# One level of Strassen's algorithm in the last output projection of a two-layer trunk, with weight sums made by GpSimd's DMAs

## Chip, cores and metric

The kernel runs on one core of a Trainium2 chip, in fp32. The metric is the device time of one execution in microseconds (us), the median of three runs. The engines are named as in the profile: PE is TensorE (PEld its weight loads), DVE VectorE, ACT ScalarE, POOL GpSimd, SP SyncE, whose queue issues DMAs.

## Reference

```python
x1 = x + gated_deltanet(rmsnorm(x, w0), ...)          # layer 0
# layer 1, Mamba-2 SSD mixer on h = rmsnorm(x1, w1):
#   z, xBC, dt = split(h @ w_in); xBC = silu(causal_conv(xBC))
#   chunked state-space scan (chunks of 128 tokens, 32 heads in 8 groups) -> y
#   y = grouped_rmsnorm(y * silu(z))                   # 1024 x 2048
x2 = x1 + y @ w_out                                    # w_out 2048 x 1024
out = rmsnorm(x2, final_w)                             # 1024 x 1024
```

1024 tokens, model width 1024, inner width 2048. The change concerns the last `y @ w_out` and what stands around it.

## The kernel before

Every large product is made from two fp32r pieces of each operand: `split` (L86, L87) writes a high piece with ACT (`scalar.copy`) and the remainder with DVE (`tensor_tensor` subtract), and three matmuls (high·high, high·low, low·high) go into one PSUM bank. A tile scheduler sorts the instructions of each engine by its own estimate; each engine then runs its list in order and waits on semaphores. Tiles come from pools with tags; a tag's buffers go round, so a new tile waits until the old one of its buffer has been read. All DMAs are issued by SP.

**Scan of layer 1.** The outer loop runs over groups g = -1 to 7. In each group 8 slots take one step of `scan(g)`, which treats one chunk n of 128 tokens, and one step of the projections and convolutions of group g+1 (`conv_halves`, whose halo COPY and MEMSET of 3 columns are POOL's L196 and L194). In a scan step `prep` uses POOL for `xw` (L861) and `t2` (L871), and `main` uses it for `S` (L887) and for the 1/rms of the group norm, `so` (L907, L909); DVE then makes `yn` (L910), PE turns `yn` in the next step's `store` (L66), ACT scales it to `yg` (L921) and SP stores it to `y1d` (L923). Where g = 7, there is no next group, and the matmuls of `out_proj` fill PE between the last steps.

**Output projection.** `out_proj` runs over halves nh of 512 output columns and 8 token tiles n; each of the 16 passes sums 16 tiles of 128 rows of w_out into one bank: 16 x 16 x 3 = 768 matmuls (L347 to L349) of 128x512. The weight pieces (`woh`, `wol`) of a half stay in SBUF; `y` is loaded and split in both halves (`yr`, `yh`, `yl`, 64 loads). In half 0 the sum with the residual `xin` (L353) is stored to DRAM (`xfd`); in half 1 it is loaded again, ACT sums the squares (L107, L113), POOL makes 1/rms (L115, L116), DVE scales the row (L119), and it is stored (L990). Layer 0 ends with the same function.

The next `with` opens a pool in the memory that the scan's pool has just left, and what is written there waits for its last readers:

```python
    with tc.tile_pool(name="nrm2", bufs=2) as nrm:
        nw = load_nw(nrm, final_norm_w)
        ...
        out_proj(yd1, sw_out, lambda n: x1d[n], (apool, bpool), nrm, nw, rows_last, xfd)
```

## Time and profile before

| what | value |
|---|---|
| median of 3 runs | 1995.43 us (1994.64 to 2000.03) |
| the profiled execution, its own time | 1990.66 us |
| its span, first to last instruction | 1989.0 us |
| mean granted clock of TensorE | 0.987 |
| PE busy | 1919.1 us, 96% |
| DVE busy | 1305.7 us, 66% |
| POOL busy | 411.6 us, 21% |

The span is 1.66 us shorter than the execution's own time, and that execution is 4.77 us faster than the median of the runs. PE's busy time counts a matmul from its start to its modelled end; matmuls overlap, so a group's mean (some 395 ns for 128x512) is longer than the distance from one to the next.

### The profile page before, as it was taken

The numbers are of one execution on the slowest core, as the hardware profiler recorded it, in microseconds if no ns is written. First come the engines' busy times: TensorE is split into PE (matmuls) and PEld (weight loads), VectorE is DVE, ScalarE is ACT, GpSimd is POOL, SyncE is SP. The second block draws the span as 40 slices with busy tenths as digits, with TensorE's granted clock in tenths as the row PEclk, the third lists the DMA queues.
The fourth block names the chain that finished last, engine by engine and source line by source line (L and its number), as shares of the span: only waits on it lengthen the run. The fifth ranks groups of instructions, "written<-read, shape, count | busy, mean of one in ns | idle before, by whom it ended". The sixth has DMA issues, their size and how long they took to land.

```text
span 1989.0 us, 36043 instructions
## 1 busy us (share of the span) xinstructions
PE 1919.1 (96%) x12974; PEld 1639.7 (82%) x12974; DVE 1305.7 (66%) x2915; ACT 1063.4 (53%) x2893; POOL 411.6 (21%) x818
## 2 busy tenths in 40 slices
PE   7997999999999999999999999999999999999998
PEld 5786888888888888897778788888888888888886
DVE  6797685778677776844354676657666676767333
ACT  5635656575656666564343554544555555555332
POOL 1101211212122212100000032423333243332000
PEclk9997999999999999999999999999999999999999
DMA  4421323232232323235574232222222223236654
GB/s 141 117 54 49 98 56 84 67 78 75 57 93 52 99 49 105 58 94 157 152 221 133 64 91 80 69 84 80 64 80 57 80 75 83 78 104 195 203 170 142
DMA packets 284789, 193.35 MB, mean 97 GB/s; under 512 B 65425, under 2 KB 246338, under 8 KB 284610
## 3 DMA queue, kind: packets, MB, share of 16 engines
q1 hardware_dynamic: 284610, 191.05, 34.2%
q8 instruction: 102, 1.67, 0.4%
q14 instruction: 77, 0.63, 0.1%
HBM read 159.34 MB, written 31.65 MB: 96 GB/s over the span
## 4 chain that ended last, share of the span: by engine, by line
PE 75%; DMA 9%; DVE 7%; ACT 4%; POOL 2%; issue 2%; SPq 1%; POOLq 0%; DVEq 0%; ACTq 0%
PE ps_proj L165 9%; PE ps_proj L166 9%; PE ps_proj L167 9%; PE ps_proj L347 6%; PE ps_proj L349 6%; PE ps_proj L348 5%; PE ps_proj L227 5%; PE ps_proj L228 4%; PE ps_proj L229 4%; DMA gcrow<-gcr_s 2%; PE ps_tr L66 2%; PE ps_pt L66 2%; DMA X<-xd 2%; DVE acc L204 2%; PE ps_sc L895 1%
## 5 line engine op out<-in xcount | busy, mean ns | idle before, releaser
L165 PE MATMUL ps_proj<-hid_h,wh 128*128 128x512 f32 x1024 | 412.9, 403 | 3.4 <-ACT acc L200 3.2
L167 PE MATMUL ps_proj<-hid_h,wl 128*128 128x512 f32 x1024 | 404.9, 395 | 0.0
L166 PE MATMUL ps_proj<-hid_l,wh 128*128 128x512 f32 x1024 | 403.6, 394 | 0.0
L227 PE MATMUL ps_proj<-zh,hid_h 128*128 128x256 f32 x1024 | 300.5, 293 | 1.0 <-DVE z L234 1.0
L229 PE MATMUL ps_proj<-zh,hid_l 128*128 128x256 f32 x1024 | 295.4, 288 | 0.0
L228 PE MATMUL ps_proj<-zl,hid_h 128*128 128x256 f32 x1024 | 295.4, 288 | 0.0
L165 PEld LDWEIGHTS ps_proj<-hid_h,wh 128*128 128x128 f32 x1024 | 192.7, 188 | 43.9 <-ACT acc L200 4.0
L167 PEld LDWEIGHTS ps_proj<-hid_h,wl 128*128 128x128 f32 x1024 | 192.5, 188 | 40.3
L166 PEld LDWEIGHTS ps_proj<-hid_l,wh 128*128 128x128 f32 x1024 | 192.9, 188 | 35.4
L347 PE MATMUL ps_proj<-woh,yh 128*128 128x512 f32 x512 | 205.2, 402 | 4.6 <-ACT yh L86 3.2
L348 PE MATMUL ps_proj<-wol,yh 128*128 128x512 f32 x512 | 204.4, 400 | 0.8 <-DVE wol L87 0.7
L349 PE MATMUL ps_proj<-woh,yl 128*128 128x512 f32 x512 | 203.1, 399 | 0.8 <-DVE yl L87 0.7
L227 PEld LDWEIGHTS ps_proj<-zh,hid_h 128*128 128x128 f32 x1024 | 196.3, 192 | 6.0 <-DVE z L234 2.3
L228 PEld LDWEIGHTS ps_proj<-zl,hid_h 128*128 128x128 f32 x1024 | 196.4, 192 | 3.0
L229 PEld LDWEIGHTS ps_proj<-zh,hid_l 128*128 128x128 f32 x1024 | 196.4, 192 | 0.3
L204 DVE SCALAR_TENSOR_TENSOR acc<-raw,cw_ssd,acc 128x512 f32<-128x512 f32 x192 | 156.5, 815 | 45.2 <-ACT acc L202 42.5
L86 ACT CAST yh<-yr 128x512 fp32r<-128x512 f32 x128 | 79.1, 619 | 142.2 <-PE ps_proj L348 90.8
L87 DVE TENSOR_TENSOR yl<-yr,yh 128x512 fp32r<-128x512 f32 x128 | 89.0, 696 | 98.7 <-ACT yh L86 98.3
L204 DVE SCALAR_TENSOR_TENSOR acc<-raw,cw_gdn,acc 128x512 f32<-128x512 f32 x192 | 145.9, 761 | 11.8 <-ACT acc L200 10.2
L87 DVE TENSOR_TENSOR wl<-wr,wh 128x512 fp32r<-128x512 f32 x128 | 89.3, 698 | 68.3 <-ACT wh L86 67.7
L317 POOL TENSOR_SCALAR_AFFINE_SELECT gcrow<-gcrow 128x512 f32<-128x512 f32 x128 | 92.1, 722 | 197.1 <-DMA gcrow<-gcr_g 141.8
L676 POOL TENSOR_SCALAR so<-so,cq 128x2 f32<-128x2 f32 x64 | 27.3, 426 | 462.7 <-ACT yn L675 462.7
(240 smaller groups left out, 3872.0 us busy)
## 6 DMA issues: line engine op xcount, KB each, us to landing
wr<-in_gdn_w_in_dram SPq DMA_DIRECT2D x96, 256.0 KB, 3.0
wr<-in_ssd_w_in_dram SPq DMA_DIRECT2D x96, 256.0 KB, 2.9
gcrow<-gcr_g SPq DMA_DIRECT2D x64, 256.0 KB, 3.6
yr<-y0d SPq DMA_DIRECT2D x64, 256.0 KB, 3.4
gcrow<-gcr_s SPq DMA_DIRECT2D x64, 256.0 KB, 3.9
yr<-y1d SPq DMA_DIRECT2D x64, 256.0 KB, 3.2
y0d<-yg SPq DMA_DIRECT2D x64, 128.0 KB, 1.9
wr<-in_gdn_w_out_dram SPq DMA_DIRECT2D x32, 256.0 KB, 3.5
```

Of the source, the lines that this page charges most:

```text
L87: nc.vector.tensor_tensor(out=lo, in0=src, in1=hi.bitcast(F32), op=ALU.subtract)
L165: nc.tensor.matmul(pt[0:nco], hi[:, j, 0:nco], xh[:, j, :], start=first, stop=False)
L166: nc.tensor.matmul(pt[0:nco], hi[:, j, 0:nco], xl[:, j, :], start=False, stop=False)
L167: nc.tensor.matmul(pt[0:nco], lo[:, j, 0:nco], xh[:, j, :], start=False, stop=last)
L204: nc.vector.scalar_tensor_tensor(out=acc, in0=raw[:, k:k + 512], scalar=cw[:, k * 32 + ti:k * 32 + ti + 1], in1=acc, op0=ALU.mult, op1=ALU ...
L227: nc.tensor.matmul(pt, xh, zh[:, k, :], start=k == 0, stop=False)
L228: nc.tensor.matmul(pt, xh, zl[:, k, :], start=False, stop=False)
L229: nc.tensor.matmul(pt, xl, zh[:, k, :], start=False, stop=k == KT - 1)
L317: nc.gpsimd.affine_select(out=t, in_=t, pattern=[[0, 4], [1, P]], compare_op=ALU.is_ge, fill=-1e30, base=0, channel_multiplier=-1)
L347: nc.tensor.matmul(pt, yh[:, j, :], hi[:, j, :], start=first, stop=False)
L348: nc.tensor.matmul(pt, yh[:, j, :], lo[:, j, :], start=False, stop=False)
L349: nc.tensor.matmul(pt, yl[:, j, :], hi[:, j, :], start=False, stop=last)
```

## The change

Layer 0 keeps the old function under the name `out_rows`. Layer 1's projection is cut into quarters: tokens into halves t, y's 2048 columns into halves k, the output columns into halves c. Instead of 8 products of quarters it makes 7 products of sums of quarters (Strassen's algorithm in Winograd's form), each of 8 steps j over 128 rows, with 4 token tiles p of 12 matmuls in a step: 7 x 8 x 12 = 672 matmuls (L427 to L429).

- **Weight sums.** `weight_sums` writes four sums of w_out's quarters to DRAM tiles `wo_ss1` to `wo_ss4`. It uses 44 DMAs issued by POOL, from DRAM to DRAM, 256x512 (512 KB) each: 16 copies (L358) and 28 that add to what is there (L360). One is issued per scan slot from group 0 on.
- **Products 0 and 1** (`early`) stand in slots 4 to 7 of group 7, with pieces in the pool of the old weight pieces. For product 1 POOL subtracts two loads of y (`N1`, L391, 8 times). ACT copies the 8 results from PSUM to `M` (L456).
- **Products 2 to 6** (`rest`) stand after the scan, in the pool `nrm2`, with rings of 4 for each piece. Products 2 and 6 make their y operand `Tt` with DVE (L394, 16 times), product 4 makes it with POOL (L387, 8 times). Results are added to the rows `xrow`, which are kept in SBUF: by POOL (`put_u`, L479, 20 times) and DVE (`put_u` 4, `grow` L482 8, `put` L473 and L475 12 times). The residual's 16 half rows are loaded over the steps of products 2 and 3 (L465).
- The store and reload of `xfd` are gone. `y1d` is laid out in four tiles, and y is loaded as 128x512.

```diff
+    def weight_sums(w_out, nm, which):
+        X = lambda c, k: w_out[k * 1024:(k + 1) * 1024, c * 512:(c + 1) * 512]
+        parts = {"s1": ((1, 0), (1, 1)), "s2": ((1, 0), (1, 1), (0, 0)), "s3": ((0, 0), (1, 0)),
+                 "s4": ((0, 1), (1, 0), (1, 1), (0, 0))}
+        forms = {f"x{c}{k}": X(c, k) for c in range(2) for k in range(2)}
+        parts = {f: parts[f] for f in which}
+        for f in parts:
+            forms[f] = tc.dram_tile([1024, 512], F32, name=f"wo_{nm}{f}")
+        def steps():
+            for q in range(4):
+                r = slice(q * 256, (q + 1) * 256)
+                for i in range(4):
+                    for f, p in parts.items():
+                        if i < len(p):
+                            src, dst = X(*p[i])[r, :], forms[f][r, :]
+                            if i == 0:
+                                d = nc.gpsimd.dma_start(dst, src)
+                            else:
+                                d = nc.gpsimd.dma_start(dst, src, accum_op=ALU.add)
+                            tc.keep_in_program_order(d)
+                            yield
+        return forms, steps()
...
+    def out_proj(yd, X, made, resid):
+        tok = lambda t, p: p + 4 * (1 - t)
+        wf = ("x00", "s1", "s2", "x01", "s3", "s4", "x11")
+        U = lambda: [ps_proj(), ps_proj(), ps_pt(), ps_pt()]
+        V = lambda: [ps_tr(), ps_tr(), ps_sc(), ps_sc()]
+        def load_y(k, t, j, tag="acc"):
+            yr = cv.tile([P, 515], F32, tag=tag, name="yr", bufs=3)[:, 0:512]
+            nc.sync.dma_start(yr, yd[k, 1 - t][j * P:(j + 1) * P, :])
+            return yr
+        def y_form(i, j, Tt):
+            if i in (0, 3, 5):
+                return load_y(*{0: (0, 0), 3: (1, 0), 5: (1, 1)}[i], j)
+            if i == 4:
+                a, b = load_y(1, 1, j), load_y(0, 1, j, "raw")
+                nc.gpsimd.tensor_tensor(out=a, in0=a, in1=b, op=ALU.subtract)
+                return a
+            if i == 1:
+                a, b, d = load_y(0, 0, j), load_y(0, 1, j, "raw"), N1[j // 4][:, j % 4, :]
+                (nc.gpsimd if made else nc.vector).tensor_tensor(out=d, in0=a, in1=b, op=ALU.subtract)
+            else:
+                a, d = load_y(*{2: (1, 1), 6: (1, 0)}[i], j), Tt[:, j, :]
+                nc.vector.scalar_tensor_tensor(out=d, in0=N1[j // 4][:, j % 4, :] if i == 2 else d, scalar=-1.0, in1=a,
+                                               op0=ALU.mult, op1=ALU.subtract)
+            return d
...
+        def pieces(i, j, ring, Tt):
+            raw = w_form(wf[i], j)
+            wh, wl, yh, yl = ring(j)
+            split(wh, wl, raw)
+            split(yh, yl, y_form(i, j, Tt))
+            return wh, wl, yh, yl
+        def mac(pt, pc, p, first, last):
+            wh, wl, yh, yl = pc
+            c = slice(p * P, (p + 1) * P)
+            nc.tensor.matmul(pt, yh[:, c], wh, start=first, stop=False)
+            nc.tensor.matmul(pt, yh[:, c], wl, start=False, stop=False)
+            nc.tensor.matmul(pt, yl[:, c], wh, start=False, stop=last)
+        def product(i, banks, ring, Tt=None):
+            for j in range(KT):
+                pc = pieces(i, j, ring, Tt)
+                for p in range(4):
+                    mac(banks[p], pc, p, j == 0, j == KT - 1)
+                yield
...
+        def early():
+            M.extend(apool.tile([P, 4, 512], F32, tag="a0", name="M", bufs=2) for _ in range(2))
+            N1.extend(apool.tile([P, 4, 512], F32, tag="a1", name="N1", bufs=2) for _ in range(2))
+            for i in range(2):
+                banks = U()
+                yield from product(i, banks, in_a(("a2", "a3") if made else ("a2",)))
+                for p in range(4):
+                    nc.scalar.copy(M[i][:, p, :], banks[p])
+        def rest(npool, nw, on_rows, before_last=lambda: None):
+            rows = {t: [npool.tile([P, D], F32, tag="xr", name="xrow", bufs=NT) for _ in range(4)] for t in range(2)}
+            Tt = npool.tile([P, 8, 512], F32, tag="T", name="Tt", bufs=1)
+            u, m = M
...
+            def ring(j):
+                return [npool.tile([P, 512], F32R, tag=t, name=t, bufs=4) for t in ("woh", "wol", "yh", "yl")]
+            def put(t, p, c, pt, op):
+                v = half(t, p, c)
+                if op == ALU.add:
+                    nc.vector.tensor_tensor(out=v, in0=pt, in1=v, op=ALU.add)
+                else:
+                    nc.vector.tensor_tensor(out=v, in0=v, in1=pt, op=ALU.subtract)
+            def put_u(t, p, c, op, of=u, eng=nc.gpsimd):
+                v = half(t, p, c)
+                eng.tensor_tensor(out=v, in0=v, in1=of[:, p, :], op=op)
+            def grow(p, pt):
+                nc.vector.tensor_tensor(out=u[:, p, :], in0=pt, in1=u[:, p, :], op=ALU.add)
...
+            def d01():
+                for p in range(4):
+                    put_u(0, p, 0, ALU.add)
+                for p in range(4):
+                    put_u(1, p, 1, ALU.subtract, m, nc.vector)
+                    put_u(1, p, 0, ALU.add, m)
+            def d2(p, pt):
+                grow(p, pt)
+                put_u(1, p, 0, ALU.add)
+            def d3(p, pt):
+                put(0, p, 0, pt, ALU.add)
+                first(0, p, 0)
+            def d4(p, pt):
+                grow(p, pt)
+                put_u(1, p, 1, ALU.subtract)
+                first(1, p, 1)
+                put_u(0, p, 1, ALU.subtract)
+            def d5(p, pt):
+                put(1, p, 0, pt, ALU.add)
+                finish(1, p, 0)
+            for i, done in ((2, d2), (3, d3), (4, d4), (5, d5)):
+                banks = V() if i % 2 else U()
+                for j, _ in enumerate(product(i, banks, ring, Tt)):
+                    if i == 2 and j < 6:
+                        for q in range(2 * j, 2 * j + 2):
+                            fetch(*((0, q, 0), (1, q - 4, 1), (1, q - 8, 0))[q // 4])
+                    if (i, j) == (2, 6):
+                        d01()
+                    if i == 3 and j < 4:
+                        fetch(0, j, 1)
+                if i == 5:
+                    before_last()
+                for p in range(4):
+                    done(p, banks[p])
+            banks = U()
+            for j in range(4):
+                pc = pieces(6, j, ring, Tt)
+                for p in range(4):
+                    mac(banks[p], pc, p, j == 0, False)
+            pcs = [pieces(6, j, ring, Tt) for j in range(4, KT)]
+            for p in range(4):
+                for j in range(4):
+                    mac(banks[p], pcs[j], p, False, j == 3)
+                put(0, p, 1, banks[p], ALU.subtract)
+                finish(0, p, 1)
...
+    def y_cut(yd, g, n):
+        return yd[g // 4, n // 4][(g % 4) * 256:(g % 4 + 1) * 256, (n % 4) * P:(n % 4 + 1) * P]
...
             for slot in range(8):
+                if g >= 0:
+                    next(steps1, None)
+                if g == 7 and slot > 3:
+                    next(early1)
+                    next(early1)
                 next(S, None)
+                if g == 7 and slot > 3:
+                    next(early1)
                 next(J, None)
             flush()
+            if g == 7:
+                next(early1)
+                next(early1)
             next(S, None)
+            for _ in early1 if g == 7 else ():
+                pass
+    bctx.close()
...
-        out_proj(yd1, sw_out, lambda n: x1d[n], (apool, bpool), nrm, nw, rows_last, xfd)
+        rest1(nrm, nw, rows_last)
```

The instructions move as follows. POOL, in one slot of group 0 of layer 1's scan, from the 1/rms of one chunk (`so`) to that of the next. Before:

```order
L909 TENSOR_TENSOR so_14272<-so_14272,expo_82 128x1
L196 COPY raw_14437<-raw_14316 128x3
L194 MEMSET raw_14565 128x3
L887 TENSOR_TENSOR S_14497<-S_14381,egl_s_13351 128x256
L871 TENSOR_TENSOR t2_14464<-xs_13459,dskip_327 128x256
L907 TENSOR_SCALAR so_14400<-so_14400 128x1
```

The same place after the change:

```order
L1140 TENSOR_TENSOR so_14269<-so_14269,expo_82 128x1
L215 COPY raw_14435<-raw_14313 128x3
L360 DMA wo_ss3_343<-in_ssd_w_out_dram 256x512
L213 MEMSET raw_14564 128x3
L360 DMA wo_ss4_344<-in_ssd_w_out_dram 256x512
L1118 TENSOR_TENSOR S_14496<-S_14379,egl_s_13343 128x256
L1102 TENSOR_TENSOR t2_14463<-xs_13451,dskip_327 128x256
L1138 TENSOR_SCALAR so_14398<-so_14398 128x1
```

Two adding DMAs stand around the halo's MEMSET, ahead of `S`, `t2` and the next `so`. The 44 DMAs stand in 22 such pairs, one DMA a slot on the average, in groups 0 to 5. In two of the pairs (rows of `wo_ss4` behind rows of `wo_ss4`) the second adds to what the first has just added to, and waits for its landing.

PE, around the last transposes of the scan (`yn`, the last chunk of group 7). Before:

```order
L349 MATMUL ps_proj_21811<-woh_21639,yl_21869 128x512
L66 MATMUL ps_tr_21572<-ident_73,yn_21567 128x128 x2
L347 MATMUL ps_proj_21888<-woh_21585,yh_21891 128x512
L348 MATMUL ps_proj_21888<-wol_21586,yh_21891 128x512
L349 MATMUL ps_proj_21888<-woh_21585,yl_21892 128x512
```

After the change (`wy` are the pieces of product 1, `woh`, `wol`, `yh` and `yl` those of product 2):

```order
L427 MATMUL ps_proj_21760<-wy_21945 128x512
L66 MATMUL ps_tr_21936<-ident_73,yn_21859 128x128 x2
L428 MATMUL ps_proj_21760<-wy_21945 128x512
...
L429 MATMUL ps_pt_21762<-wy_21969 128x512
L427 MATMUL ps_proj_22011<-woh_22017,yh_22019 128x512
L428 MATMUL ps_proj_22011<-wol_22018,yh_22019 128x512
L427 MATMUL ps_proj_22012<-woh_22017,yh_22019 128x512
L428 MATMUL ps_proj_22012<-wol_22018,yh_22019 128x512
L427 MATMUL ps_pt_22013<-woh_22017,yh_22019 128x512
L428 MATMUL ps_pt_22013<-wol_22018,yh_22019 128x512
L429 MATMUL ps_proj_22011<-woh_22017,yl_22020 128x512
```

Where the old order goes on with matmuls whose operands are of the old pools, the new one has 20 matmuls of product 1 left, and then the first of product 2, whose pieces lie in the new pool.

DVE at the same place. Before:

```order
L903 TENSOR_TENSOR y_21560<-y_21560,z7_20965 128x256
L87 TENSOR_TENSOR wol_22061<-wr_22062,woh_22060 128x512
L910 TENSOR_SCALAR yn_21567<-y_21560,so_21566 128x256
L87 TENSOR_TENSOR wol_22061<-wr_22066,woh_22060 128x512
L87 TENSOR_TENSOR wol_22061<-wr_22070,woh_22060 128x512
L87 TENSOR_TENSOR yl_21892<-yr_21889,yh_21891 128x512
```

After the change:

```order
L1141 TENSOR_SCALAR yn_21859<-y_21852,so_21858 128x256
L87 TENSOR_TENSOR wy_21969<-N1_21437,wy_21969 128x512
L394 SCALAR_TENSOR_TENSOR Tt_22010<-N1_21436,yr_22023 128x512
L394 SCALAR_TENSOR_TENSOR Tt_22010<-N1_21436,yr_22050 128x512
L394 SCALAR_TENSOR_TENSOR Tt_22010<-N1_21436,yr_22077 128x512
L87 TENSOR_TENSOR wol_22018<-wr_22015,woh_22017 128x512
L87 TENSOR_TENSOR wol_22045<-wr_22042,woh_22044 128x512
L87 TENSOR_TENSOR wol_22072<-wr_22069,woh_22071 128x512
L87 TENSOR_TENSOR wol_22099<-wr_22096,woh_22098 128x512
L87 TENSOR_TENSOR yl_22020<-Tt_22010,yh_22019 128x512
```

Three sums and four weight remainders stand ahead of the first `yl` of product 2. `Tt`, `woh` and the rows are in the new pool, so the first write there on DVE, on ACT (`woh_22017`), on POOL (`xrow`, L479) and the load of `nw` on SP wait for the landing of the last stores of `y1d`, which read `yg` from the old pool. After that landing ACT's order is four `woh`, one copy to `M`, then `yh_22019`.

## Rows read from the trace of the kernel before

**Rows 1.** The page, sections 1 and 4: busy time, chain that ended last.

```profile
PE 1919.1 (96%) x12974; PEld 1639.7 (82%) x12974; DVE 1305.7 (66%) x2915; ACT 1063.4 (53%) x2893; POOL 411.6 (21%) x818
...
PE 75%; DMA 9%; DVE 7%; ACT 4%; POOL 2%; issue 2%; SPq 1%; POOLq 0%; DVEq 0%; ACTq 0%
```

**Rows 2.** Windows: PE, PEld, DVE, ACT, POOL busy (count), clock, DMA share, GB/s.

```profile
1200.00:1740.00 540.00, 536.33 (x3708) 461.21 (x3707) 358.13 (x658) 281.44 (x742) 180.48 (x331) 1.00 0.27 76
...
1795.50:1840.00 44.50, 44.50 (x253) 35.86 (x252) 34.15 (x65) 26.10 (x63) 7.93 (x16) 1.00 0.69 210
1840.00:1981.60 141.60, 141.60 (x615) 115.09 (x613) 54.90 (x83) 43.78 (x85) 7.22 (x22) 1.00 0.59 177
```

**Rows 3.** Chain of waits at the end: start, us, what.

```profile
1981.98 0.70 DVE xrow L359
...
1984.46 0.75 DVE xn L119
1985.22 0.66 DVEq L990
```

**Rows 4.** Groups by line, 1750 to 1989 us: busy, mean ns | idle before.

```profile
L87 DVE TENSOR_TENSOR yl<-yr,yh 128x512 fp32r<-128x512 f32 x64 | 45.0, 703 | 55.6 <-ACT yh L86 55.5
L86 ACT CAST yh<-yr 128x512 fp32r<-128x512 f32 x64 | 39.6, 619 | 72.6 <-PE ps_proj L348 57.2 <-issue 10.6 <-DMA yr<-y1d 3.1
L87 DVE TENSOR_TENSOR wol<-wr,woh 128x512 fp32r<-128x512 f32 x32 | 22.6, 727 | 11.6 <-ACT woh L86 11.4
...
L119 DVE SCALAR_TENSOR_TENSOR xn<-xrow,rr,nw 128x512 f32<-128x512 f32 x16 | 11.3, 748 | 10.2 <-POOL rr L116 10.2
...
L359 DVE TENSOR_TENSOR xrow<-ps_proj,xin 128x512 f32<-128x512 f32 x8 | 5.5, 692 | 14.3 <-PE ps_proj L349 14.3
```

**Rows 5.** Timeline, the scan's last store: start, us, engine line.

```profile
1837.40 0.38 PE L66 MATMUL ps_tr<-ident,yn 128*128 128x128 f32 x2
...
1839.21 0.61 ACT L921 ACTIVATE yg<-ps_tr,vecs 128x128 f32<-128x128 f32 x2
...
1839.92 0.42 SPq L923 DMA_DIRECT2D y1d<-yg  x1
```

**Rows 6.** DMA issues, 1200 to 1740 us: count, KB, median us to landing.

```profile
gcrow<-gcr_s SPq DMA_DIRECT2D x52, 256.0 KB, 3.9
y1d<-yg SPq DMA_DIRECT2D x50, 128.0 KB, 1.8
```

**Rows 7.** DMA issues, 1790 to 1989 us.

```profile
y1d<-yg SPq DMA_DIRECT2D x6, 128.0 KB, 3.4
```

**Rows 8.** Windows (as Rows 2) at the start of layer 0's output projection.

```profile
1008.90:1010.40 1.50, 0.13 (x2) 0.07 (x1) 0.09 (x1) 0.74 (x2) 0.00 (x0) 1.00 0.96 192
1010.50:1013.80 3.30, 3.30 (x8) 2.39 (x9) 1.80 (x3) 0.92 (x2) 0.00 (x0) 0.50 0.95 313
```

**Rows 9.** Timeline of POOL over one scan step: [idle before, releaser].

```profile
1363.70 0.10 POOL L194 MEMSET raw<- 128x3 f32 x1
1366.80 0.95 POOL L861 TENSOR_TENSOR xw<-xs,dtd_s 128x256 f32<-128x256 f32 x1 [3.00 <-PE ps_sc L882]
...
1368.34 0.61 POOL L871 TENSOR_TENSOR t<-xs,dskip 128x256 f32<-128x256 f32 x1
1370.92 0.19 POOL L907 TENSOR_SCALAR so<-so 128x1 f32<-128x1 f32 x1 [1.97 <-ACT yn L906]
```

**Rows 10.** Timeline of DVE's convolution sums while POOL is idle.

```profile
1407.12 2.33 DVE L204 SCALAR_TENSOR_TENSOR acc<-raw,cw_ssd,acc 128x512 f32<-128x512 f32 x3 [2.39 <-ACT acc L202]
```

**Rows 11.** Timeline, the same sums beside POOL's work.

```profile
1430.10 2.81 DVE L204 SCALAR_TENSOR_TENSOR acc<-raw,cw_ssd,acc 128x512 f32<-128x512 f32 x3
...
1430.22 1.12 POOL L317 TENSOR_SCALAR_AFFINE_SELECT gcrow<-gcrow 128x512 f32<-128x512 f32 x1
...
1431.31 1.05 POOL L861 TENSOR_TENSOR xw<-xs,dtd_s 128x256 f32<-128x256 f32 x1
```

**Rows 12.** View of the tile `so`, 1200 to 1750 us: who waited.

```profile
PE ps_tr L66: 3.6, 5
```

More of the change, by code (lines that the diff above doesn't have):

```diff
@@ L102, in rms_rows, with rms_first, rms_second, rms_first0 @@
         return xn
-    def rms_first(pool, xrow):
+    def rms_first(sq, xrow, c):
+        ss = st.tile([P, 2], F32, tag="ss8", name="ss8", bufs=NT)
+        nc.scalar.activation(sq, xrow[:, c * 512:(c + 1) * 512], AF.Square, accum_out=ss[:, 0:1])
+        nc.gpsimd.tensor_scalar(out=ss[:, 0:1], in0=ss[:, 0:1], scalar1=1.0 / D, scalar2=EPS, op0=ALU.mult,
+                                op1=ALU.add)
+        return ss
+    def rms_second(xrow, xn, ss, nw, emit, c):
+        cs = slice(c * 512, c * 512 + 512)
+        nc.scalar.activation(xn[:, cs], xrow[:, cs], AF.Square, accum_out=ss[:, 1:2])
+        r = st.tile([P, 1], F32, tag="rr", name="rr")
+        nc.gpsimd.tensor_scalar(out=r, in0=ss[:, 1:2], scalar1=1.0 / D, scalar2=ss[:, 0:1], op0=ALU.mult, op1=ALU.add)
+        nc.gpsimd.tensor_tensor(out=r, in0=r, in1=neg_half[:, 0:1], op=ALU.pow)
+        for kh in range(2):
+            cs = slice(kh * 512, kh * 512 + 512)
+            nc.vector.scalar_tensor_tensor(out=xn[:, cs], in0=xrow[:, cs], scalar=r, in1=nw[:, cs], op0=ALU.mult,
+                                           op1=ALU.mult)
+            emit(kh, xn[:, cs])
+    def rms_first0(pool, xrow):
         xn = pool.tile([P, D], F32, tag="xn", name="xn")
@@ L399, in hybrid_trunk, with y_dram @@
     dskip = bcast(ssd_d[0], 32, "dskip")
+    def y_dram(nm):
+        return {(k, t): tc.dram_tile([1024, 512], F32, name=f"{nm}{k}{t}") for k in range(2) for t in range(2)}
+    def y_cut(yd, g, n):
+        return yd[g // 4, n // 4][(g % 4) * 256:(g % 4 + 1) * 256, (n % 4) * P:(n % 4 + 1) * P]
     yd0 = [tc.dram_tile([2048, P], F32, name=f"y0d{n}") for n in range(NT)]
+    yd1 = y_dram("y1d")
+    wo1, steps1 = weight_sums(sw_out, "s", ("s1", "s2", "s3", "s4"))
+    early1, rest1 = out_proj(yd1, wo1, True, lambda n: x1d[n])
     with tc.tile_pool(name="gw", bufs=2) as gw:
@@ L785, in hybrid_trunk @@
                 z_weights(g + 1)
-    bpool = ctx.enter_context(tc.tile_pool(name="bpool", bufs=2))
+    bctx = ExitStack()
+    bpool = bctx.enter_context(tc.tile_pool(name="bpool", bufs=2))
     hid2 = hid_tiles(apool)
@@ L796, in rows_mid @@
             norm(lambda kh, xn: to_hid(kh, xn, hid2, n))
-        out_proj(yd0, gw_out, lambda n: x[n * P:(n + 1) * P, :], (apool, bpool), nrm, nw, rows_mid, x1d)
-    yd1 = [tc.dram_tile([2048, P], F32, name=f"y1d{n}") for n in range(NT)]
-    xfd = [tc.dram_tile([P, D], F32, name=f"xfd{n}") for n in range(NT)]
+        out_rows(yd0, gw_out, lambda n: x[n * P:(n + 1) * P, :], (apool, bpool), nrm, nw, rows_mid, x1d)
     with tc.tile_pool(name="sw", bufs=2) as sw:
```

46 lines of the change are left out of this document (41 added, 5 removed).

## The prediction

> **What bounds the kernel now.** I read the page first: PE is busy for 96% of the span and holds 75% of the chain that ended last [rows 1]. The average hides stages, so I cut the end into windows [rows 2]. Up to 1740 us the scan of layer 1 keeps PE busy for 536.33 of 540 us; from 1795.5 us, where the projection's matmuls begin between the last scan steps, PE has no gap at all. From 1840 to 1981.6 us it issues 615 instructions in 141.6 us at the full clock of 1.00, which is 141.6 / 615 = 0.2302 us for each 128x512 matmul. In the same window DVE works for 54.9 us (39%), POOL for 7.2, DMA is at 0.59. So here only PE counts, and a matmul left out is worth 0.2302 us as long as all else keeps up. Last I read the chain's end [rows 3]: after the last matmul the row's last half passes DVE, ACT, POOL, DVE and SP from 1981.98 to the span's end at 1989.0, 7 us, which no matmul covers.
>
> **Matmuls.** 768 become 672: 96 x 0.2302 = **-22.1 us**. This is the whole gain; all other parts cost.
>
> **The handoff from product 1 to product 2.** Before, nothing is written to new memory at this point, and PE goes on without a gap. After, the first writes of product 2 wait for the landing of the scan's last store. Its time comes from two places. In the timeline the last transposes start at 1837.40, ACT's two `yg` end at 1839.82, and SP issues the store at 1839.92 [rows 5]: 2.5 us from transposes to issue, of which ACT is busy with splits for about 1.4, so 1.1 to 2.5. From issue to landing such a store takes 1.8 us in the scan [rows 6] and 3.4 us under the projection's loads [rows 7]. The landing S then lies 2.9 to 5.9 us after the transposes; I take 4.2, a little under the middle, since the loads of y for product 2 are mostly done by then. ACT needs six operations of 0.62 us [rows 4] from S to the end of the first `yh`: S + 3.7. PE has 20 matmuls left when the transposes are done, 20 x 0.23 = 4.6 us. The idle time is 4.2 + 3.7 - 4.6 = **+3.3 us** (2.0 to 5.0). DVE is not far behind: three `Tt` (the nearest row, L119, has 748 ns), four remainders of 727 ns and one of 703 give the first `yl` at S + 5.9; PE's order puts six matmuls without `yl` ahead, which covers 1.4 of those 2.2 us.
>
> What a pause like this does to the clock stands in layer 0, at the start of its projection: PE had only 0.13 us of work in 1.5 us, and the next 3.3 us ran at a granted clock of 0.50, that is at 1.2 GHz instead of 2.4 [rows 8]. 3.3 us at half speed lose about 1.7 us; a part of it falls together with the wait for `yl`, so the two give **+1.7 us** (0 to 3).
>
> **Feeding products 2 to 6.** They last 480 x 0.2302 = 110.5 us. DVE's work in them, by the rows of 4: 80 splits x 0.715 = 57.2; 16 `Tt` and 16 row scalings x 0.748 = 23.9; 24 sums of the size of L359 x 0.692 = 16.6; together 97.7 us, 88% where it was 39% in the window before. POOL makes 28 sums of 128x512. No such row is shown; the nearest is 0.61 us for a 128x256 sum [rows 9], so twice that, 1.2 us alone, 34 us in all. DVE and POOL slow each other: three convolution sums take 2.33 us while POOL is idle [rows 10], and 2.81 beside 2.17 us of POOL work [rows 11], 0.22 us for each us of POOL. That adds 34 x 0.22 = 7.5 us to DVE: 105 of 110.5 us. It still fits, but the load is uneven. In product 6 the eight `Tt`, 16 splits, eight scalings and four sums are 26 us against 22.1 of PE; rings of four steps and product 5's slack cover some of it. The DMAs are near their limit in product 2 as well: `nw` (0.5 MB) and six half rows (1.6 MB) are issued ahead of the fourth load of y, some 2.1 MB, or 6.7 us at the 313 GB/s that a full queue moved [rows 8], and after it every step wants 1 MB in 2.76 us. Between nothing, if the rings cover all of it, and 10 us, if product 6's excess of 4 and a DMA delay of some 6 both show, I take **+4 us**.
>
> The Trainium skill speaks against this part: by "SBUF — State Buffer", section "Who interferes with whom", DVE and GpSimd share one pair of ports as an exclusive lock, and a DVE instruction with two SBUF inputs contends with a GpSimd instruction that reads SBUF. The rows agree in kind (2.33 to 2.81 us), but show 0.22 of POOL's time and not all of it; what the whole lock would cost is rival 5.
>
> **Products 0 and 1 in the last slots.** Their 192 matmuls fill PE as the old ones did there. They need 32 splits, as many as the old stretch had for as many matmuls, but also 8 copies on ACT (5 us), 8 sums on POOL (9.6 us alone, beside a POOL that was busy for 7.93 of 44.5 us [rows 2]) and 24 loads of y. POOL's sums stand ahead of `so` of the last chunks. **+2 us** (0 to 6).
>
> **The 44 DMAs of POOL in the scan.** No DMA of POOL and no adding DMA is shown before. In a scan step POOL is idle for 3.00 us behind the halo's MEMSET, where a pair goes, and for 1.97 us before `so` [rows 9]. The nearest row for the issue itself is SP's, 0.42 us [rows 5]; by it a pair of 0.84 us is hidden, and so it is up to 1.5 us for each; the operations behind it (`xw`, `S`, `t2`) are needed late, but `so` leads to `yn`, to PE's transposes and to the next step. Two pairs have a second member that waits for the first one's landing: 3.9 us, if it is as long as the row of gcrow [rows 6]. Their 22.5 MB to read and as much to write join a DMA share of 0.27 [rows 2]. Lower bound 0; a gain is excluded, since nothing is taken away from the scan. Upper bound: every pair holds POOL as long as such a landing, 0.9 us longer than the idle stretch, 22 x 0.9 = 20 us. SP's issue is the row of the same kind, so I stay near the lower end: **+2 us**, the two waits (2 x 0.9).
>
> **The tail.** The last quarter's halves finish per token tile as before, with the sum, the square, 1/rms and the scaling in the same order [rows 3], but DVE has up to six scalings of earlier rows between. **+1 us** (0 to 2).
>
> **Sum.** -22.1 + 3.3 + 1.7 + 4 + 2 + 2 + 1 = -8.1. The sum is made against the profiled execution: 1990.66 - 8.1 = 1982.6 us. That execution lies 4.77 below the median of the runs, 1995.43, so the forecast for the median is **1987.4 us** (-0.4%).
>
> **Rivals.**
> 1. *Main case*, the sum above: 1982 to 1992 us, chance 0.46.
> 2. *DVE and the loads become the bound.* If product 6's excess shows whole (4), product 2 waits for DMA (6), and the early slots cost 6, the terms are -22.1 + 5 + 10 + 6 + 2 + 1 = +1.9; with a part of it covered, 1993 to 1998 us, no measurable change. For it: 105 of 110.5 us; against it: rings of four, and ACT and DMA have room on the mean. 0.21.
> 3. *Slower: POOL's DMA pairs delay `so`.* If a pair holds POOL for longer than the idle 3.00 us, the excess goes into `xw` and `so`, behind them into `yn` and PE's in-order transposes, 22 times. The gain is gone at 8.1 / 22 = 0.37 us per pair beyond the main case, and it is measurably slower from 0.64. At 1 us per pair: 1987.4 + 22 = 2009 us. For it: PE already waits for `yn` at five places, 3.6 us [rows 12]; against it: POOL was busy for just 180 of 540 us. 0.14. It could also come from DVE's side: if each DMA waited behind one DVE instruction of 0.75 us (L119's), a pair would be 1.5 us later, and the idle stretch would cover it only where an issue costs less than 0.75 us. The Trainium skill names this way ("SBUF — State Buffer", section "🔬 SBUF: two separate sides", its warning on DMAs issued from GpSimd): GpSimd writes their descriptors, and a DVE instruction in a two-port mode locks it out. No row of before has such a DMA.
> 4. *All is covered.* The handoff's 5 us remain, the rest is hidden: 1995.43 - 22.1 + 5 = 1978 us. 0.15.
> 5. *POOL blocks DVE wholly* in products 2 to 6 instead of for 0.22 of its time: 97.7 + 34 = 131.7 us of DVE, 21 us more than PE's 110.5, in place of the 4 us of the sum: 1987.4 - 4 + 21 = 2004 us. Against it: [rows 10, 11], where it is 0.48 us beside 2.17. 0.04.
>
> **Chances and range.** A measurement tells 0.3%, 6 us, from no change. Faster, below 1989.4: case 4 (0.15) and most of the main case (0.41): 0.56. Same: the rest of the main case (0.05) and case 2: 0.26. Slower: cases 3 and 5, 0.18. The range goes from case 4's 1977 to 2000, past case 2; what it leaves out is case 5, most of case 3 and a little below case 4, 0.2. The main case's own range is 1982 to 1992.
>
> **What would show it.** Right: 672 matmuls; a gap of 2 to 5 us of PE just before L427's first matmul of product 2, released by ACT's `yh`, then a clock of about 0.5 for a few us; products 2 to 6 in 110 to 121 us with DVE near 90%; the scan up to group 6 within 4 us of before. Wrong: PE idle before L66 with the release by `yn` in groups 0 to 5 (case 3), `xw` or `so` standing behind a POOL DMA; or gaps within products 2 to 6 ended by `yl`, `Tt` or a load of y (case 2).

## The result, and the profile after

The changed kernel takes 1981.46 us (median of 17 runs, 1979.31 to 1994.54), the kernel before, run beside it, 1996.43 (17 runs, 1987.66 to 2003.13). The ratio is 0.9933, 95% interval 0.9918 to 0.9948. The forecast was 1987.4 us, a gain of 8 us; the measured one is 13 us by the ratio, at the lower edge of the main case's 1982 to 1992 us.

The page of the profiled execution (1979.31 us, span 1977.5 us): busy time, the chain that ended last, the new queue, and POOL's DMAs with their median us to landing.

```profile
PE 1891.2 (96%) x12878; PEld 1616.0 (82%) x12878; DVE 1361.1 (69%) x2955; ACT 1072.4 (54%) x2917; POOL 508.3 (26%) x898
...
q0 software_dynamic: 9920, 23.07, 6.3%
...
PE 69%; DVE 10%; DMA 9%; POOL 4%; ACT 4%; issue 3%; SPq 0%; POOLq 0%; DVEq 0%; ACTq 0%
...
wo_ss<-in_ssd_w_out_dram POOLq DMA_DIRECT2D x44, 512.0 KB, 6.6
```

PE has 96 instructions less than in [rows 1] and 28 us less of busy time, but DVE has 55 us more and POOL 97, and DVE's share of the last chain went from 7 to 10%. To see where the rest went, both traces are cut at the same four places: first state matmul of the scan, first matmul of the last projection, last matmul, end. The kernel before (columns as in [rows 2]):

```profile
0.00:1164.00 1164.00, 1105.52 (x7701) 947.33 (x7702) 798.33 (x1997) 663.52 (x1874) 183.04 (x387) 0.98 0.35 94
1164.00:1795.50 631.50, 627.12 (x4412) 541.39 (x4410) 416.22 (x769) 329.27 (x871) 212.63 (x391) 1.00 0.27 77
...
1795.50:1982.00 186.50, 186.44 (x866) 150.96 (x864) 89.07 (x148) 69.88 (x148) 15.15 (x38) 1.00 0.61 184
...
1982.00:1989.00 7.00, 0.00 (x0) 0.00 (x0) 2.09 (x3) 0.72 (x2) 0.81 (x2) 0.83 0.20 75
```

The changed kernel:

```profile
0.00:1156.60 1156.60, 1098.12 (x7704) 942.32 (x7705) 797.30 (x1997) 663.04 (x1874) 185.16 (x389) 0.98 0.35 96
1156.60:1793.15 636.55, 628.38 (x4407) 541.75 (x4405) 425.96 (x767) 328.01 (x869) 245.29 (x433) 0.99 0.46 113
...
1793.15:1965.95 172.80, 164.66 (x770) 131.94 (x768) 132.33 (x186) 79.92 (x172) 75.53 (x72) 1.00 0.63 208
...
1965.95:1977.50 11.55, 0.00 (x0) 0.00 (x0) 5.47 (x9) 1.44 (x4) 2.34 (x5) 0.67 0.47 182
```

The scan is 5.05 us longer, the projection 13.7 us shorter, the tail 4.55 us longer: 4.1 us in all behind the scan's start. The other 7.4 us of the difference between these two profiles lie ahead of the scan, in 1156 us of layer 0 and the start of layer 1, which the change does not touch. There TensorE's granted clock was at its lower level, 1.2 GHz, for 51.2 us before and for 37.6 us after (summed over windows of 1 us); half of the difference, 6.8 us, is an estimate of what that is worth at most.

In the projection the matmuls gave what they should: 866 - 770 = 96, and 186.5 - 22.1 = 164.4 us would be left. The waits of PE from the last slots on say where 8.1 of the missing 8.4 us went (total, times, longest):

```profile
PE ps_proj L427 <- ACT yh L86: 3.5, 2, 2.7
PE ps_tr L66 <- DVE yn L1141: 1.6, 1, 1.6
PE ps_proj L428 <- DVE wol L87: 1.4, 3, 0.6
PE ps_proj L427 <- issue: 1.3, 1, 1.3
PE ps_pt L427 <- ACT M L456: 0.3, 1, 0.3
```

The two last rows are the handoff. Its timeline, and the window around its gap:

```profile
1843.13 0.38 PE L66 MATMUL ps_tr<-ident,yn 128*128 128x128 f32 x2
...
1844.25 0.37 SPq L1154 DMA_DIRECT2D y1d<-yg  x1
...
1846.11 2.18 ACT L86 CAST woh<-wr 128x512 fp32r<-128x512 f32 x4 [1.89 <-DMA y1d<-yg]
...
1849.39 0.47 PE L427 MATMUL ps_proj<-woh,yh 128*128 128x512 f32 x1 [1.30 <-issue]
```

```profile
1848.10:1851.00 2.90, 1.34 (x5) 0.76 (x6) 2.90 (x6) 2.90 (x7) 0.00 (x0) 1.00 0.82 232
```

The store is issued 1.1 us after the transposes start and has landed 1.9 us later: both near the lower ends of the ranges. The view names no releaser for the first matmul of product 2; it starts 0.1 us after ACT's first `yh` ends, at 1849.30. PE is idle for 1.3 us, and its clock stays at 1.00.

What DVE and POOL do in the products stands in the groups by line, 1845 to 1966 us:

```profile
L87 DVE TENSOR_TENSOR wol<-wr,woh 128x512 fp32r<-128x512 f32 x40 | 32.2, 813 | 0.0
L87 DVE TENSOR_TENSOR yl<-yr,yh 128x512 fp32r<-128x512 f32 x24 | 24.7, 1033 | 11.2 <-ACT yh L86 6.4 <-PE ps_sc L429 2.9 <-PE ps_sc L428 1.8
...
L479 DVE TENSOR_TENSOR xrow<-xrow,M 128x512 f32<-128x512 f32 x4 | 5.2, 1327 | 1.9 <-DMA xrow<-x1d 1.9
L473 DVE TENSOR_TENSOR xrow<-ps_tr,xrow 128x512 f32<-128x512 f32 x4 | 2.7, 684 | 0.0
...
L479 POOL TENSOR_TENSOR xrow<-xrow,M 128x512 f32<-128x512 f32 x20 | 31.6, 1607 | 35.6 <-DVE M L482 20.2 <-ACT M L456 14.3 <-DMA xrow<-x1d 1.0
```

The 24 `yl` from loaded y went from 703 to 1033 ns, `wol` from 727 to 813 [rows 4]. DVE's sums of two SBUF tiles take 1327 ns, those with one operand in PSUM (L473) 684, no more than L359 in [rows 4]. At one place both kinds stand beside the same POOL sums:

```profile
1877.55 2.54 POOL L479 TENSOR_TENSOR xrow<-xrow,M 128x512 f32<-128x512 f32 x2 [12.17 <-DVE M L482]
...
1877.92 1.28 DVE L482 TENSOR_TENSOR M<-ps_pt,M 128x512 f32<-128x512 f32 x2
1879.12 1.52 DVE L87 TENSOR_TENSOR wol<-wr,woh 128x512 fp32r<-128x512 f32 x1
```

Two sums with an operand in PSUM take 1.28 us together, one `wol` with both inputs in SBUF takes 1.52. By the Trainium skill, "SBUF — State Buffer", section "Who interferes with whom", a DVE instruction with two SBUF inputs contends with a GpSimd instruction that reads SBUF, and one with at most one SBUF input, outside the two-port modes, does not; L87 beside L482 agrees.

In the scan, PE waits for `yn` for 7.8 us in all, before for 4.3. The largest gap lies at 1383 us. 18 us ahead of it a DMA holds up POOL:

```profile
1365.25 0.90 POOL L360 DMA_DIRECT2D wo_ss<-in_ssd_w_out_dram  x1 [2.41 <-DVE y L1134]
1365.84 0.95 POOL L1118 TENSOR_TENSOR S<-S,egl_s 128x256 f32<-128x256 f32 x1
...
1382.85 1.06 POOL L336 TENSOR_SCALAR_AFFINE_SELECT gcrow<-gcrow 128x512 f32<-128x512 f32 x1 [1.44 <-DMA gcrow<-gcr_s]
1383.89 0.18 POOL L1138 TENSOR_SCALAR so<-so 128x1 f32<-128x1 f32 x1
```

This L360 is the second member of one of the two pairs that wait for their first, issued at 1358.92; that one took 6.0 us to land, so the releaser that the view names, DVE's `y`, was hardly what it waited for. `S` and `so` stand behind it. The chain that the profile follows back from the gap does not pass this DMA: it goes over a load of weights issued at 1367.95, which stands in it for 4.1 us (median landing 2.9), and the last gcrow at 1377.38, with 5.4 (median 3.9); `so` stands behind that row's select on POOL, and PE waits for `yn`. That the pair shifted these loads no row shows; that the gap goes with the pair, a run below shows.

```profile
PE ps_tr L66 <- DVE yn L1141: 2.2, 1, 2.2
```

Behind this gap the granted clock is at its lower level, 1.2 GHz, for 3.4 us, and so it is for 3.4 us behind a gap of 2.1 us at 1207, where the kernel before has one of 0.6; in the kernel before it never is between the scan's start and the last matmul:

```profile
1386.10:1389.50 3.40, 3.40 (x19) 2.70 (x16) 2.96 (x6) 1.31 (x4) 0.60 (x1) 0.50 1.10 259
```

The other thing that changed in the scan is landing. In the window 1160 to 1480 us:

```profile
wo_ss<-in_ssd_w_out_dram POOLq DMA_DIRECT2D x30, 512.0 KB, 6.6
...
y1d<-yg SPq DMA_DIRECT2D x29, 128.0 KB, 3.9
```

A store of `y1d` lands in 3.9 us instead of 1.8 [rows 6]; the medians of the loads, 2.9 us for weights and 3.9 for gcrow, are those of before.

The end of the chain shows why the tail grew:

```profile
1967.27 1.34 DVE xn L119 x2
...
1968.62 2.03 DMA out_dram<-xn
...
1970.75 0.63 ACT xn L113
...
1972.76 0.75 DVE xn L119
```

The last row's square (L113) writes into `xn`, which has two buffers, and waits 2 us for the store of an earlier row to land. Before, the last rows' sums (L359) came 11.2 us apart; now the four last (L475) stand within 4 us, from 1962.77 to 1966.59.

### The profile page after: what moved, and what is told of

Same layout as the page of the kernel before. It is cut to its first block, busy times and chain, and to the rows that moved or that the text cites. A ratio compares the mean times of both kernels' runs of the same rounds, so it can differ in the third digit from the quotient of the medians.

```text
span 1977.5 us, 36053 instructions
## 1 busy us (share of the span) xinstructions
PE 1891.2 (96%) x12878; PEld 1616.0 (82%) x12878; DVE 1361.1 (69%) x2955; ACT 1072.4 (54%) x2917; POOL 508.3 (26%) x898
## 4 chain that ended last, share of the span: by engine, by line
PE 69%; DVE 10%; DMA 9%; POOL 4%; ACT 4%; issue 3%; SPq 0%; POOLq 0%; DVEq 0%; ACTq 0%
PE ps_proj L184 9%; PE ps_proj L185 8%; PE ps_proj L186 8%; PE ps_proj L246 5%; PE ps_proj L248 4%; PE ps_proj L247 4%; DMA gcrow<-gcr_s 3%; PE ps_proj L571 3%; PE ps_proj L572 2%; PE ps_proj L573 2%; DVE acc L223 2%; PE ps_tr L66 2%; PE ps_pt L66 2%; DMA X<-xd 2%; PE ps_sc L867 1%
## 5 line engine op out<-in xcount | busy, mean ns | idle before, releaser
L223 DVE SCALAR_TENSOR_TENSOR acc<-raw,cw_ssd,acc 128x512 f32<-128x512 f32 x192 | 160.8, 838 | 43.4 <-ACT acc L221 40.6
L87 DVE TENSOR_TENSOR wl<-wr,wh 128x512 fp32r<-128x512 f32 x128 | 90.3, 706 | 61.6 <-ACT wh L86 60.8
L203 ACT ACTIVATE th<-acc 128x512 f32<-128x512 f32 x128 | 80.1, 627 | 85.2 <-DVE acc L223 85.1
L718 DVE TENSOR_TENSOR tm<-Dt,X 128x2 f32<-128x2 f32 (+30 forms) x248 | 87.0, 351 | 46.6 <-POOL X L707 41.7
L216 ACT COPY raw<-ps_proj 128x512 f32<-128x512 f32 x128 | 74.3, 581 | 80.3 <-PE ps_proj L186 75.8
L86 ACT CAST wh<-wr 128x512 fp32r<-128x512 f32 x128 | 78.7, 616 | 68.5 <-PE ps_proj L185 56.9
L571 PE MATMUL ps_proj<-woh,yh 128*128 128x512 f32 x256 | 103.0, 403 | 5.9 <-ACT yh L86 4.6
```

The costliest lines, as they stand in the source:

```text
L87: nc.vector.tensor_tensor(out=lo, in0=src, in1=hi.bitcast(F32), op=ALU.subtract)
L203: nc.scalar.activation(th, src, AF.Tanh, scale=0.5)
L223: nc.vector.scalar_tensor_tensor(out=acc, in0=raw[:, k:k + 512], scalar=cw[:, k * 32 + ti:k * 32 + ti + 1], in1=acc, op0=ALU.mult, op1=ALU ...
L571: nc.tensor.matmul(pt, yh[:, j, :], hi[:, j, :], start=first, stop=False)
L718: nc.vector.tensor_tensor(out=tv, in0=Dt[:, r0:, s:], in1=X[:, s:s + 1, s:].to_broadcast([P, nr, nj]), op=ALU.mult)
```

## The experiments

"Scan", "projection" and "tail" are the three stretches of the windows above. For the kernel before they are 631.5, 186.5 and 7.0 us, for the changed one 636.6, 172.8 and 11.6.

**Both kernels once more.** No edit.

> The changed kernel once more, unaltered, for the length of its stages. In the first profile the stretch ahead of layer 1's scan was 7 to 8 us shorter than before, although its instructions are the same. Theory A (the change's own terms explain the whole difference, and the stretch ahead of the scan only varies from run to run): here it lies anywhere between the two, and the stages behind it repeat within 1 us: scan start to first matmul of product 0 636.5 us, last transposes to last matmul 122.4 us, last matmul to the end 11.6 us. Theory B (the change shortens the stretch ahead of the scan too): it is again 7 to 8 us shorter than in the kernel before.

> The kernel before once more, for the spread of its stages. In the three profiles with the changed kernel's code the stretch ahead of layer 1's scan took 1156.6, 1169.4 and 1167.8 us, in the one profile of the kernel before 1164.0. Theory A (this stretch only varies): it lies between 1155 and 1171 us here, and the stages behind it repeat: 631.5, 42.3, 144.2 and 7.0 us, each within 1 us. Theory B (the kernel before is slower in that stretch, or its profile was a lucky one in the scan): it is above 1171 us, or the scan is longer than 633 us.

The changed kernel: 636.7, 171.9 and 11.7 us, with 1169.4 us ahead of the scan; ratio 0.9952 (0.9935 to 0.9969). The kernel before: 631.5, 186.7 and 7.0 us, with 1169.0 ahead. In these pairs the later stages repeat within 1 us; the stretch ahead of the scan varies. Over all twelve profiles of the changed kernel and its variants it lies between 1156.6 and 1169.4 us, 1163.8 on the mean, over the two of before at 1164.0 and 1169.0, mean 1166.5. So the profiles favour theory A, but do not refute theory B: the median spans beside this run, 1995.8 us before (11 runs) and 1985.4 after (8), less the 825.0 and 820.3 us of the stages from the scan on, leave 1170.8 and 1165.1 us ahead of it, if those stages are as long in every run. By that some 6 us of the gain lie ahead of the scan, and why is open.

The later stages do not always repeat so well. Six profiles whose projection does the same work (the two above and the runs without weight sums, with spread ones, with tiny ones and with four `xn`) give 171.6 to 176.1 us for it, with 3.3 to 5.5 us of waits in products 2 to 6 and 0 to 6.8 us at 1.2 GHz. A difference inside these bounds says nothing.

**Weight sums left out.**

```diff
-            forms[f] = tc.dram_tile([1024, 512], F32, name=f"wo_{nm}{f}")
+            forms[f] = X(*parts[f][0])
...
-        return forms, steps()
+        return forms, iter(())
```

> The 44 DMAs of POOL are left out, and the products read plain quarters of the weights in place of the sums, so the output is not the reference's. Theory A (the DMAs cost the scan its 5 us, by holding POOL or by their traffic): scan start to first matmul of product 0 is 631 to 633 us instead of 636.5, without gaps of 2 us before the transposes of yn, and the time is 4 to 6 us lower than the changed kernel's. Theory B (the gaps come from loads of gcrow and of weights that collide in SP's queue, as they already did before): 635 to 637 us, two or more gaps of 1 to 2 us are left, and the time moves by less than 2 us.

```profile
1167.80:1799.50 631.70, 626.55 (x4412) 541.15 (x4410) 414.36 (x767) 328.02 (x869) 211.86 (x391) 1.00 0.27 79
```

The scan takes 631.7 us, as before the change, and the gap of 2.2 us in group 2 is gone: the DMAs cost the scan its 5 us. But gaps of 1.85 and 1.0 us at the ends of groups 0 and 1 are left; the kernel before has gaps at the same places, of 0.6 to 0.9 and 1.4 to 1.5 us. The ratio to before, 0.9937 (0.9917 to 0.9957), does not tell it from the changed kernel; the median is 2.6 us lower than that kernel's beside it, not the 4 to 6 of theory A.

**The same DMAs in an order without waiting pairs.**

```diff
-                for i in range(4):
-                    for f, p in parts.items():
-                        if i < len(p):
+                for f, i in (("s4", 0), ("s1", 0), ("s2", 0), ("s4", 1), ("s3", 0), ("s1", 1), ("s4", 2), ("s2", 1),
+                             ("s3", 1), ("s4", 3), ("s2", 2)):
...
```

> The same 44 DMAs in another order, in which no DMA adds to the rows that its neighbour in the pair has just written. Theory A (the 5 us of the scan come from the one pair in group 2 whose second member holds POOL until the first has landed): scan start to first matmul of product 0 is 631 to 633 us, and the gap of 2 to 3 us near 1383 to 1394 us is gone. Theory B (the traffic of the DMAs or their issue delays the loads in the queue): 635 to 637 us, and that gap stays.

```profile
PE ps_tr L66 <- DVE yn L1140: 0.3, 1, 0.3
```

```profile
1164.30:1798.25 633.95, 625.95 (x4408) 539.24 (x4406) 421.79 (x767) 329.00 (x871) 245.84 (x434) 1.00 0.47 113
1798.25:1974.30 176.05, 167.59 (x769) 134.22 (x768) 131.44 (x185) 80.37 (x172) 74.93 (x72) 0.98 0.63 204
```

The gap in group 2 shrinks from 2.2 us to 0.3, as theory A says; in the eight profiles with the old order it is 1.5 to 3.0 us. The scan takes 634.0 us, between the two theories and inside the 633.3 to 638.7 us of those eight (mean 635.8), so what the pair is worth in the scan is not shown. PE still waits for `yn` for 7.7 us in all; what is gone are the 6.8 us at half clock, and as much of it stands in the projection instead, behind gaps of 2.2 and 2.8 us. The other waiting pair, in group 5 (its second member starts at 1608.70 in the first profile), is followed by no gap of PE over 0.25 us up to 1720 us.

**DMAs of 4 rows in place of 256**, with products that read plain quarters.

```diff
-                r = slice(q * 256, (q + 1) * 256)
+                r = slice(q * 256, q * 256 + 4)
...
```

> The 44 DMAs stay where they are, but each moves 4 rows instead of 256 and the products read plain quarters of the weights, so the output is not the reference's. Theory A (what the scan loses beside the waiting pair is POOL's time for issuing, 0.6 to 0.95 us for each): scan start to first matmul of product 0 is 633.5 to 636 us. Theory B (it is the traffic in the DMA engines): 631.5 to 632.5 us, as without the DMAs; a waiting pair hardly costs, since its first member lands in some 2 us instead of 6.

```profile
1162.60:1793.40 630.80, 625.17 (x4408) 539.49 (x4406) 419.53 (x767) 327.94 (x869) 244.58 (x433) 1.00 0.28 79
```

```profile
y1d<-yg SPq DMA_DIRECT2D x29, 128.0 KB, 1.8
wo_ss<-in_ssd_w_out_dram POOLq DMA_DIRECT2D x30, 8.0 KB, 2.2
```

POOL still issues 44 DMAs and is as busy as with the large ones (244.6 against 245.3 us), yet the scan takes 630.8 us and the stores land in 1.8 us again: theory B, 0.7 us below its range, in one profile. Issuing costs nothing here; what costs goes with the bytes, the traffic or the wait inside a pair, which this run takes away together.

**Rows two steps later, nw in product 3**, and the first sums into the rows (`d01`) one step later.

```diff
-                    if i == 2 and j < 6:
-                        for q in range(2 * j, 2 * j + 2):
+                    if i == 2 and j > 1:
+                        for q in range(2 * j - 4, 2 * j - 2):
...
-                    if (i, j) == (2, 6):
+                    if (i, j) == (2, 7):
```

> The load of nw is moved into product 3, and the 12 half rows of product 2 are issued two steps later, behind the loads of y that the next steps want. Theory A (the 4.0 us that PE waits in product 2 come from loads of y that stand behind 2 MB of rows and nw): the waits of product 2 fall from 4.0 to under 1 us, last transposes to last matmul from 122.4 to 118.5 us. Theory B (DVE, slowed by POOL's sums, is what is late): the waits stay at 3 to 4 us and end with Tt or yl instead.

```profile
PE ps_proj L429 <- DVE yl L87: 1.4, 1, 1.4
...
PE ps_proj L428 <- DVE wol L87: 0.6, 2, 0.3
```

The waits for late loads are gone, but 1.4 us before `yl` came in their place: the rows land earlier, so POOL's sums start beside DVE's first splits. The waits of products 2 to 6 are 2.0 us, but behind the gaps of 1.3 and 1.4 us stand 6.8 us at 1.2 GHz: from the last transposes to the last matmul 121.1 us, not the 118.5 of theory A, and the projection 171.3 us, hardly less than the six above. Neither theory alone.

**Rows from step 3 on.** As above, from j = 3.

> The 12 half rows of product 2 are issued from step 3 on. Theory A (loads of y late behind the rows; and the gap of 1.4 us before yl that came when the rows landed earlier was DVE slowed by POOL's first sums): no gap before yl, waits of product 2 under 1 us beside the 1.3 us of the handoff, last transposes to last matmul 117 to 119.5 us. Theory B (DVE cannot keep up with product 2 in any order): some 2 us of waits for Tt, yl or wol remain, 121 us or more.

The gap before `yl` is gone, and 0.8, 2.0 and 0.6 us before `wol` and `yl` in the middle of product 2 took its place; projection 171.9 us, 121.5 behind the last transposes. Theory B: moving the loads moves the wait.

**POOL's 20 sums into the rows left out.**

```diff
-                eng.tensor_tensor(out=v, in0=v, in1=of[:, p, :], op=op)
+                if eng is nc.vector:
+                    eng.tensor_tensor(out=v, in0=v, in1=of[:, p, :], op=op)
```

> POOL's 20 sums into the rows (L479) are left out, so the output is not the reference's. Theory A (POOL's sums slow DVE, 0.2 to 0.3 us for each us, but the rings cover it): yl and wol come back to some 0.70 to 0.73 us from 1.03 and 0.82, but last transposes to last matmul falls by less than 1.5 us from 122. Theory B (the shared port is what PE waits for): it falls by 3 us or more, with no waits for Tt, yl or yh in product 2.

```profile
1796.85:1964.40 167.55, 164.18 (x770) 133.55 (x768) 118.49 (x186) 80.86 (x172) 43.55 (x52) 0.99 0.64 215
```

```profile
PE ps_proj L427 <- issue: 1.3, 1, 1.3
PE ps_pt L427 <- ACT M L456: 0.3, 1, 0.3
```

Only the handoff is left of PE's waits behind the last transposes, although nw and the rows are still loaded ahead of y, and the projection takes 167.6 us, 4 us under the lowest of the six. From the last transposes (end 1848.8) to the last matmul it is 115.6 us with the same 501 matmuls, 6.8 less than in the first profile. Theory B: POOL's sums are what PE waits for. DVE's busy time is 118.5 us, 13.8 less than in the first profile and 10.8 to 14.0 less than in the six: 0.5 to 0.7 us for each sum taken from POOL.

**The sums spread over products 2, 3 and 4**: 4, 8 and DVE's 4, with their loads.

```diff
                     if (i, j) == (2, 6):
-                        d01()
-                    if i == 3 and j < 4:
+                        for p in range(4):
+                            put_u(0, p, 0, ALU.add)
+                    if i == 3:
+                        fetch(1, j % 4, j // 4)
+                        if j > 3:
+                            put_u(1, j - 4, 0, ALU.add, m)
+                            put_u(1, j - 4, 0, ALU.add)
+                    if i == 4 and j < 4:
+                        put_u(1, j, 1, ALU.subtract, m, nc.vector)
...
```

> POOL's sums into the rows are moved out of product 2 where they can: 4 stay there, 8 go to product 3 with their rows' loads, and DVE's 4 go to product 4; nw is loaded in product 4. Theory A (PE's waits in product 2 come from POOL's 8 sums beside DVE's heaviest stretch, by the port, and from the rows ahead of the loads of y): last transposes to last matmul 116 to 118.5 us, no wait of product 2 over 0.5 us but the handoff's 1.3 us. Theory B (the sums cost PE the same wherever they stand, since DVE's total is too large): 120 us or more, with the waits in product 3 or 4.

Product 2 waits for 0.4 us beside the handoff, and products 3 and 4 for 1.25, 0.4 and 1.4 us instead, with 3.4 us at half the clock behind, and 3.4 more behind the wait for `yn`; projection 175.0 us, 122.9 behind the last transposes. One profile, as theory B says: the waits moved with the sums, and their total, 3.5 us, and the projection stay inside the bounds of the six.

**Four buffers for xn.**

```diff
- ... npool.tile([P, D], F32, tag="xn", name="xn"), ...
+ ... npool.tile([P, D], F32, tag="xn", name="xn", bufs=4), ...
```

> The rows' output tile xn gets four buffers instead of two. Theory A (the tail is 4 us longer than before because the last row's square waits until an earlier row's store has landed and given its buffer back): last matmul to the end falls from 11.6 to 8 or 9 us, time 3 us lower. Theory B (DVE's queue of scalings is what makes the tail long): 11 us remain.

```profile
1973.44 0.69 DVE xrow L475
...
1974.15 0.63 ACT xn L113
```

The square follows the sum at once, and the tail is 9.2 us, 2.4 less, where the profiles with two buffers have 11.3 to 12.5: theory A. The ratio, 0.9937 (0.9915 to 0.9959), is too coarse for it, and the projection was 174.4 us here.

**All three together** (spread rows, spread weight sums, four buffers).

> The balanced rows, four buffers for xn and the spread order of the weight sums together. If the three causes are separate, the stages are those of each alone: scan start to first matmul of product 0 633 to 636 us, last transposes to last matmul 116 to 118.5, last matmul to the end 9 to 9.5; together about 8 us under the changed kernel, ratio to the kernel before some 0.990 to 0.991. Rival: what is won is given back as waits for yn and half clock elsewhere, ratio 0.993 or more.

Scan 633.2 and tail 9.2 us as expected, projection 175.3, 122.6 behind the last transposes; ratio 0.9945 (0.9926 to 0.9964). The outcome is the rival's: the projection has 2.3 us before `yn`, four waits of 0.6 to 1.7 us for the splits and 6.8 us at 1.2 GHz. Since 175.3 us lies inside the bounds of the six, it shows that spreading the rows won nothing there, not that the winnings of scan and tail were its price.

**POOL's 20 sums on DVE.**

```diff
-            def put_u(t, p, c, op, of=u, eng=nc.gpsimd):
+            def put_u(t, p, c, op, of=u, eng=nc.vector):
```

> POOL's 20 sums into the rows (L479) are made by DVE instead; nothing is left out. In the profiles so far DVE was busy for 108.7 us between last transposes and last matmul with POOL's sums and for 94.0 us without them. Theory A (the two engines lock each other out, so that a sum on POOL costs DVE as much, 14.7 / 20 = 0.74 us, as making it itself, 0.69 us): DVE is busy for 107 to 109 us, last transposes to last matmul takes 121 to 123 us, and the time is that of the changed kernel within 2 us. Theory B (POOL's sums slow DVE only now and then, and moving them loads DVE more): DVE 112 us or more, the stretch 124 us or longer.

```profile
1797.50:1967.70 170.20, 164.88 (x770) 133.46 (x768) 128.91 (x204) 80.70 (x172) 45.71 (x50) 0.99 0.65 212
```

```profile
PE ps_proj L429 <- DVE yl L87: 1.2, 1, 1.2
```

(The 108.7 and 94.0 us of the expectation are sums of the single instructions' times; the windows, which count overlaps once, give 132.3 and 118.5 for the whole projection.) With 18 instructions more in the projection (204 against 186; two scalings fall behind it, and the tail is 12.5 us), DVE is busy for 128.9 us, where the six with POOL's help have 129.3 to 132.5, and only 1.2 us of waits are left in products 2 to 6, where 3.3 to 5.5 were. From the last transposes to the last matmul it is 117.4 us, less than either theory expected. Theory A in its mechanism: the help cost DVE at least as much as the work. Ratio 0.9931 (0.9909 to 0.9952), against 0.9933 and 0.9952 for the changed kernel: not slower.

## Why the prediction was right, and where not

| term | forecast | measured in the first profile |
|---|---|---|
| 96 matmuls | -22.1 | -22.1 |
| handoff, idle | +3.3 | +1.6 |
| handoff, half clock | +1.7 | 0 |
| feeding products 2 to 6 | +4 | +4.9 |
| last slots | +2 | +1.6 |
| DMAs in the scan | +2 | +5.1 |
| tail | +1 | +4.6 |
| sum | -8.1 | -4.3 |

The direction, the range and the matmuls' share were right. Of the forecast's own signs, 672 matmuls and a length of products 2 to 6 between 110 and 121 us came (116.6); the scan within 4 us (5.1), the fall of the clock at the handoff and DVE near 90% (81% from the last transposes on) did not, and signs of both case 2 and case 3 did: gaps inside product 2 that end with late splits, and PE idle before L66 in groups 0 to 2. The stages' sum of -4.3 us (windows: -4.1, and -4.8 for the second profile of the changed kernel) is smaller than the time's gain of 9.6 to 13.4 us by the two ratios. The rest seems to lie in the stretch ahead of the scan: about 3 us by the means of its 2 and 12 profiles, some 6 by the median spans. Why instructions that the change does not touch should take less time stays open, so this part of the gain is not explained. That the forecast lies near the measured time is in part chance: the stages gave half of its 8 us, a stretch that it does not mention the rest.

- *Handoff.* The step was right (first write into new memory behind the last store, ACT's order), its time was sized too long: the landing came 3.0 us after the transposes, not the 4.2 taken, since ACT was free and the store took 1.9 us; ACT's six operations then took 3.2 us, not 3.7. The forecast counted the landing from the transposes' start and PE's 20 matmuls from their end, 0.4 us apart. PE paused for 1.3 us without a fall of the clock, so the second term vanished here; half clock came behind gaps in the scan, where the forecast had none.
- *Feeding.* The size was near, the make-up was not. The forecast took 0.22 us of DVE for each us of POOL from convolution sums; here 31.6 us of POOL's sums cost DVE 10.8 to 14, 0.34 to 0.44 for each. What rival 5 names, DVE held up by POOL, is the mechanism, at a part of its price: in the rows shown it strikes DVE's instructions with two SBUF inputs and not those with one in PSUM. The 2.1 MB ahead of the loads of y play a part only together with it: without POOL's sums the same loads made nobody wait.
- *Scan.* The term was the waits of two pairs, 0.9 us each. One pair is followed by 2.2 us of idle PE and 3.4 us of half clock, the other by nothing, so the price per pair was no fixed one. Rival 3 named POOL's time for issuing; tiny DMAs showed that it costs nothing. The traffic, which the forecast named and did not price, makes the stores of `y1d` land late; how much of the 5 us goes through it and how much through the pair is open.
- *Tail.* The forecast looked at DVE's queue and missed the ring of two `xn` buffers: 2.4 of the 4.6 us. Most of the other 2.2 can be read in the run with four buffers: the last sum starts 0.7 us after the last matmul, behind scalings of earlier rows (at once before [rows 3]), and POOL's two operations of 1/rms take 2.1 us beside DVE's scalings, before 0.8.
